# Weight sums of a seven-product MLP made by adding DMAs, with a new order of products, loads and last sums

## The chip, the cores and the metric

The kernel runs on one core of one Trainium2 chip. The metric is the device time of one execution in microseconds (us); the kernel before takes 2369.47 us in the median of three runs. A core has five engines that run their own instruction streams in order and signal each other by semaphores: TensorE (PE, with PEld for its weight loads), VectorE (DVE), ScalarE (ACT), GpSimd (POOL) and SyncE (SP), which here only issues DMAs.

## The reference

Two layers of a decoder over 1024 tokens of width 1024 in float32. Each layer is a mixer (RG-LRU and retention in layer 0, HGRN2 and gated DeltaNet in layer 1) and then an MLP, both behind an RMSNorm with adaLN shift, scale and gate. The change concerns the two MLPs alone:

```python
def squared_relu_mlp(h, w1, w2):
    return jnp.square(jax.nn.relu(h @ w1)) @ w2

    # in each layer, after the mixer:
    h = modulate(rmsnorm(x, norm_mlp_w[layer]), sh_f, sc_f)
    x = x + gt_f[:, None, :] * squared_relu_mlp(h, mlp_w1[layer], mlp_w2[layer])
```

`w1` is 1024 x 4096, `w2` is 4096 x 1024. The result is x after both layers and a last RMSNorm.

## The kernel before

**Order of the work.** Nothing is issued as it is written. A `Recorder` collects every operation with its engine, an assumed duration and the tiles that it reads and writes; `place()` then plays a list schedule over all of it (per engine the ready operation with the lowest priority number, which is its place in the text plus the `bias` in force), gives each tile a buffer, and `emit()` (L333, the call itself is L342, hence one line in all rows of the profile) issues each engine's operations in that order. So what is fixed on the chip is the order per engine and the buffers; a wait at the head of an engine's stream holds up all behind it. Pools: `heap` (73 tiles of 128 x 512), `raw` (4 of 128 x 1024, loaded weights), `w` (6 of 128 x 1024, split weights), `pad` (4 of 128 x 515), `blk` (3), and in PSUM `dps` (3 banks) and `psum` (5 banks). `raw`, `w`, `blk`, `pad` and `dps` are handed out in the order of the text. All DMAs go out on SP's queue (`dma`, L476).

**Precision.** Every factor is split in two float32r tiles: hi is ScalarE's rounded copy, lo the remainder, which VectorE (or GpSimd) forms by a subtraction. A product of two factors is three matmuls: hi x hi, hi x lo, lo x hi (`mm3`, and the same written out in the MLP). `factor` (L597) splits a weight block into one `w` buffer, `operand` (L791) an activation tile into two heap tiles.

**The MLP** (`mlp`, L854). Both products are done by the seven-product scheme of Strassen and Winograd for 2 x 2 blocks: seven block products, named P1 to P7, in place of eight, with sums of blocks before and after. The tokens are cut in two halves (f = 0, 1) and the inner dimension in two; the 4096 hidden channels are 32 units of 128, taken as 16 pairs (`NP`).

- *Up* (first product). `winograd_operands` (L823) forms seven sets of four activation operands, 56 heap tiles: P1 and P2 from the first half of the tokens alone, the others from sums of both halves. `up(s, kind)` (L865) is one product: 12 matmuls of 128 x 512. P2 accumulates on P1's PSUM bank, P3 on P5's and P4 on P7's. VectorE and ScalarE form the four results (r11, r22, r12, r21) of a pair from them, apply ReLU and square, form the second product's sums t1, r, t2 and t4 of them, and spill seven tiles per pair to DRAM (`h_spill`). `mlp_plan` (L675) orders the products: P1 of the first three pairs (`LEAD`), P2 of these, their other five, then pair by pair, the last two pairs interleaved.
- *Down* (second product). `todo` (L933) goes over groups of four pairs (`GRP`), over the kinds in `DOWN_ORDER` (P1 P2 P6 P7 P4 P5 P3), over the pairs of the group; each step is again 12 matmuls, into four PSUM banks that accumulate over the four pairs. At the end of a kind, its four banks are added into x (`add_to`, L950) or into four shared tiles in two `blk` buffers, which are added into x at the very end (`last_adds`, L953). `load_h` (L937) brings the spilled tiles back six steps ahead.

**Weights.** `units` lists all weight units in the order of use; `pop` keeps three of them pushed ahead, at a priority before everything else. For the up product, `up_factor` (L619) loads two tiles of 128 x 1024 per pair into `raw` (blocks a11, a12 and a21, a22), and GpSimd forms the block sums that P5, P6, P7 and P3 need: x = a21 + a22 in a `pad` tile, then x - a11, a11 - a21, a12 - x. For the down product, `load_w` (L942) loads four blocks per pair for a whole group at once, and `down_factor` (L643) forms the same four sums on GpSimd, which there also forms the lo parts of P7, P4 and P3.

`pop` also feeds, among the up units of the first MLP, loads of adaLN weights into `raw` tiles and their multiplication on VectorE (`ada_unit`, L729), whose results the second layer needs.

The tiles of x are spilled before the MLP and loaded again in four batches of four by `X_LOADS` (L443, used at L990).

## Time and profile before

| | |
|---|---|
| runs, us | 2365.61, 2370.98, 2369.47 (median 2369.47) |
| the profiled execution's own time, us | 2369.33 |
| its span in the profile, us | 2367.6 |
| mean granted TensorE clock | 0.987 of full |
| DMA queues | one data queue, SP's: 336.80 MB in 168964 packets, 43.6% of 16 engines' span |

The stages of interest, by the trace: first MLP from about 452 us (its last operands are still being formed) to the seam between up and down at 780 to 787 us, and on to about 1090; second MLP from about 1715 us over the seam at 2032.6 to 2039.9 us to about 2347; then the last norm and the stores.

How to read the rows. A group's row gives line, engine, operation, the tile written and the tiles read, shapes and count, then busy time in us, mean duration of one in ns, and after the second bar the idle time of the engine just before these instructions, with the engines that ended it. In the timeline a row is a run of like instructions: start, length, engine, what, count, and in brackets the idle time ahead of it. In the table of windows each engine's busy time stands with its count of instructions, then granted clock, DMA share of 16 engines, GB/s. Matmuls overlap, so a matmul's mean of some 390 ns is longer than the distance between two. A few per cent of the matmul records are missing from the trace.

### The profile page before, as it was taken

Reading aid. Unit: us, or ns where it says so; the run is one execution under the profiler, and the core shown is the slowest. Engines: PE = TensorE matmul, PEld = TensorE weight load, DVE = VectorE, ACT = ScalarE, POOL = GpSimd, SP = SyncE. Lnnn points to the kernel's source line nnn. Section 1 sums busy time; section 2 is a strip of 40 time slices with the busy share of each in tenths; the row PEclk is TensorE's granted clock in tenths of the full one; section 3 lists DMA queues with packets and bytes.
Section 4 is the critical chain, followed back from the end, with each engine's and each line's share of the span. In section 5 each row is a group of like instructions: output and inputs, shape, how many; then the busy total and the mean of one; then the engine's idle time right before and its main releaser. Section 6 shows DMA issues by size and latency. Waiting matters only on the chain.

```text
span 2367.6 us, 31238 instructions
## 1 busy us (share of the span) xinstructions
PE 2291.4 (97%) x10906; PEld 1872.5 (79%) x10906; DVE 1835.2 (78%) x2719; ACT 1270.4 (54%) x2372; POOL 749.0 (32%) x695
## 2 busy tenths in 40 slices
PE   7999999999999899999999999999989999899997
PEld 4887888777778788887887888888868888788885
DVE  7997666798886788789977686656697665787787
ACT  6786463654445434445755665555465445444443
POOL 3000000123244356531164444520033332466541
PEclk8999999999999999999999999999999999999998
DMA  8333426237776845324212122234325445764431
GB/s 288 89 107 107 125 89 231 98 122 267 256 246 230 306 154 178 105 96 138 75 36 76 60 62 65 57 110 150 126 76 191 147 147 195 273 203 134 138 98 72
DMA packets 169122, 338.80 MB, mean 143 GB/s; under 512 B 26818, under 2 KB 37634, under 8 KB 168964
## 3 DMA queue, kind: packets, MB, share of 16 engines
q1 hardware_dynamic: 168964, 336.80, 43.6%
q8 instruction: 86, 1.41, 0.2%
q14 instruction: 72, 0.59, 0.1%
HBM read 254.39 MB, written 82.35 MB: 142 GB/s over the span
## 4 chain that ended last, share of the span: by engine, by line
PE 77%; DVE 9%; issue 5%; DMA 4%; ACT 4%; POOL 1%; SPq 0%; DVEq 0%; POOLq 0%; ACTq 0%
PE dps L342 41%; PE psum L342 36%; DVE heap L342 6%; ACT heap L342 3%; DMA raw<-in_dram 2%; DVE w L342 2%; DMA heap<-in_dram 1%; DVE raw L342 1%; POOL pad L342 1%; POOL raw L342 1%; ACT w L342 1%; DMA h_spill<-heap 0%; DMA d_full<-blk 0%; SPq L342 0%; DMA heap<-d_full 0%
## 5 line engine op out<-in xcount | busy, mean ns | idle before, releaser
L342 PE MATMUL dps<-heap,w 128*128 128x512 f32 x5016 | 1246.4, 395 | 5.8 <-ACT heap L342 2.8
L342 PEld LDWEIGHTS dps<-heap,w 128*128 128x128 f32 x5016 | 927.1, 188 | 197.5 <-ACT heap L342 5.2
L342 PE MATMUL psum<-heap,w 128*128 128x512 f32 x3816 | 906.4, 393 | 33.2 <-DVE heap L342 22.1
L342 PEld LDWEIGHTS psum<-heap,w 128*128 128x128 f32 x3816 | 720.8, 190 | 195.5 <-DVE heap L342 24.4
L342 DVE TENSOR_TENSOR heap<-heap,heap 128x512 f32<-128x512 f32 (+1 forms) x799 | 654.6, 847 | 90.7 <-ACT heap L342 86.4
L342 ACT ACTIVATE heap<-heap 128x512 f32<-128x512 f32 (+2 forms) x1055 | 613.6, 608 | 176.7 <-DVE heap L342 161.6
L342 ACT ACTIVATE w<-raw 128x512 fp32r<-128x512 f32 (+1 forms) x312 | 233.2, 750 | 351.2 <-PE psum L342 180.6
L342 DVE TENSOR_TENSOR w<-raw,w 128x512 fp32r<-128x512 f32 (+1 forms) x309 | 294.2, 955 | 106.2 <-ACT w L342 101.3
L342 POOL TENSOR_TENSOR pad<-raw 128x512 f32<-128x512 f32 x32 | 44.5, 1391 | 779.0 <-ACT w L342 399.0
L342 ACT ACTIVATE w<-heap 128x512 fp32r<-128x512 f32 x160 | 101.2, 632 | 242.7 <-PE psum L342 240.0
L342 POOL TENSOR_TENSOR w<-heap,w 128x512 fp32r<-128x512 f32 x96 | 137.7, 1437 | 199.7 <-ACT w L342 196.2
L342 POOL TENSOR_TENSOR blk<-blk,blk 32x31 f32<-32x31 f32 (+15 forms) x248 | 177.0, 714 | 37.2 <-DMA blk<-n_full 19.7
L342 DVE TENSOR_TENSOR heap<-psum,heap 128x512 f32<-128x512 f32 x153 | 103.7, 684 | 42.1 <-PE psum L342 41.3
L342 ACT ACTIVATE heap<-psum 128x512 f32<-128x512 f32 (+6 forms) x189 | 89.6, 481 | 82.0 <-PE psum L342 80.9
L342 PE MATMUL psum<-heap,heap 128*128 128x128 f32 (+4 forms) x1064 | 129.9, 263 | 2.2 <-DVE heap L342 2.2
L342 PEld LDWEIGHTS psum<-heap,heap 128*128 128x128 f32 (+2 forms) x1064 | 112.5, 168 | 23.5 <-DVE heap L342 5.6
L342 DVE SCALAR_TENSOR_TENSOR raw<-raw,blk 128x1024 f32<-128x1024 f32 x80 | 100.9, 1261 | 29.3 <-DMA raw<-in_dram 28.8
L342 DVE SCALAR_TENSOR_TENSOR heap<-dps,mod,heap 128x512 f32<-128x512 f32 x80 | 57.4, 747 | 55.3 <-PE dps L342 55.3
L342 POOL TENSOR_TENSOR pad<-pad,raw 128x512 f32<-128x512 f32 x32 | 51.0, 1595 | 135.8 <-DVE w L342 135.8
L342 ACT ACTIVATE heap<-dps 128x512 f32<-128x512 f32 (+1 forms) x134 | 77.5, 585 | 24.5 <-PE dps L342 14.9
L342 DVE SCALAR_TENSOR_TENSOR heap<-psum,mod,heap 128x512 f32<-128x512 f32 x112 | 78.6, 744 | 14.9 <-PE psum L342 14.7
L342 DVE TENSOR_TENSOR w<-pad,w 128x512 fp32r<-128x512 f32 x64 | 63.1, 987 | 33.3 <-ACT w L342 32.8
(174 smaller groups left out, 1533.6 us busy)
## 6 DMA issues: line engine op xcount, KB each, us to landing
raw<-in_dram SPq DMA_DIRECT2D x232, 512.0 KB, 3.7
h_spill<-heap SPq DMA_DIRECT2D x224, 256.0 KB, 3.4
heap<-h_spill SPq DMA_DIRECT2D x224, 256.0 KB, 2.9
heap<-in_dram SPq DMA_DIRECT2D x194, 256.0 KB, 5.4
x_spill<-heap SPq DMA_DIRECT2D x48, 256.0 KB, 2.0
heap<-x_spill SPq DMA_DIRECT2D x48, 256.0 KB, 5.3
heap<-g_rows SPq DMA_DIRECT2D x16, 256.0 KB, 4.4
out_dram<-heap SPq DMA_DIRECT2D x16, 256.0 KB, 2.7
```

What stands on the lines that cost most here:

```text
L342: op.call(*a, **k)
```

## The change

- **Adding DMAs.** A new helper `dma_add` issues a DMA from GpSimd's queue that adds what it reads in DRAM to the destination tile in SBUF. In the up product, per pair: a21 is loaded into the `pad` tile x by SP, a22 is added to it (P5); a21 and a22 are loaded into `raw`, a11 is added to the first (P7); a11 is added to x after P5's split has read it (P6); a12 is added to x after P6's split (P3). That is four adding DMAs and one more plain load of 256 KB per pair; GpSimd's four additions go. In the down product, a21 + a22 and a21 + a11 are formed by adding DMAs while loading (five tiles per pair in place of four), and two additions stay on GpSimd. A DMA can add but not subtract, so the scheme's first block row is taken with the other sign: some sums after the products become differences, P3's weights are split negated, and `gn` holds the negated gate.
- **All lo parts on VectorE.** `factor` no longer takes an engine.
- **Second product over 8 pairs.** `GRP` is 8: two groups of eight pairs, so PSUM is read out half as often.
- **Five pairs ahead.** `mlp_plan` begins with P1 of five pairs (`AHEAD`), then P2 of these; their a11 and a12 are loaded as separate half tiles.
- **Weights and x one by one.** `W_LOADS` names the step of a group at which each block of each pair is loaded (from eight steps before the group on), `X_LOADS` the step for each tile of x.
- **Last sums of results later.** The sums t1, r, t2, t4 of the last two pairs, and their spills, get a priority 300 places later.
- The last sums of the shared tiles into the second half of x come after P7 of the last group instead of after P4.

The diff, cut to its core:

```diff
-GRP = 4
+GRP = 8
+LATER = 300
-X_LOADS = {(0, 1): (0, 0), (1, 3): (1, 4), (2, 3): (0, 4), (3, 3): (1, 0)}
+X_LOADS = {i + n * m: (f, k + m) for i, n, f, k in ((2, 2, 0, 0), (23, 2, 1, 4), (32, 1, 0, 4), (40, 1, 1, 0)) for m in range(4)}
+W_LOADS = {(i + n * j, name): j for i, n, name in ((-8, 1, "a11"), (0, 1, "a12"), (1, 2, "x"), (10, 2, "a21"), (24, 1, "a22"))
+           for j in range(GRP)}
+AHEAD = 5
+    def dma_add(o, i, after=()):
+        n = 8 * width(o) * o.shape[0]
+        views = [x for x in (i, o) if isinstance(x, View)]
+        return rec.add("POOL", nc.gpsimd.dma_start, 800, (o, i), dict(accum_op=ALU.add), [o], views, after, n)
...
-    def factor(src, eng):
+    def factor(src, negative=False):
         w = rec.tile("w", F32R)
         hi, lo = w[:, 0:HT], w[:, HT:D]
-        act(hi, src, AF.Copy)
-        eng.tensor_tensor(lo, src, hi.bitcast(F32), ALU.subtract)
+        if negative:
+            act(hi, src, AF.Copy, scale=-1.0)
+            V.scalar_tensor_tensor(lo, src, -1.0, hi.bitcast(F32), ALU.mult, ALU.subtract)
+        else:
+            act(hi, src, AF.Copy)
+            V.tensor_tensor(lo, src, hi.bitcast(F32), ALU.subtract)
         return hi, lo
...
     def up_factor(l, s, kind, pw):
+        a11, a12 = w_1[l, 2 * s][:, 0:HT], w_1[l, 2 * s][:, HT:D]
+        a21, a22 = w_1[l, 2 * s + 1][:, 0:HT], w_1[l, 2 * s + 1][:, HT:D]
         def get():
+            if s < AHEAD and kind in ("P1", "P2"):
+                r = rec.tile("raw")[:, 0:HT]
+                dma(r, a11 if kind == "P1" else a12)
+                return factor(r)
             if kind == "P1":
-                pw["r"] = r = rec.tile("raw")
+                r = rec.tile("raw")
                 dma(r, w_1[l, 2 * s])
-                pw["a11"], pw["a12"] = r[:, 0:HT], r[:, HT:D]
+                pw["P1"], pw["P2"] = r[:, 0:HT], r[:, HT:D]
             if kind == "P5":
+                pw["x"] = padded()[:, 0:HT]
+                dma(pw["x"], a21)
+                dma_add(pw["x"], a22)
                 r = rec.tile("raw")
                 dma(r, w_1[l, 2 * s + 1])
-                pw["a21"], pw["a22"] = r[:, 0:HT], r[:, HT:D]
-                pw["x"] = padded()[:, 0:HT]
-                G.tensor_tensor(pw["x"], pw["a21"], pw["a22"], ALU.add)
...
+                pw["P7"], pw["P4"] = r[:, 0:HT], r[:, HT:D]
+                dma_add(pw["P7"], a11)
             if kind == "P6":
-                G.tensor_tensor(x, x, a11, ALU.subtract)
-            if kind == "P7":
-                G.tensor_tensor(a21, a11, a21, ALU.subtract)
+                dma_add(pw["x"], a11)
             if kind == "P3":
-                G.tensor_tensor(a12, a12, x, ALU.subtract)
...
+                dma_add(pw["x"], a12)
+            return factor(pw.get(kind, pw.get("x")), kind == "P3")
...
     def mlp_plan():
-        r = [(s, k) for k in ("P1", "P2") for s in range(LEAD)]
+        r = [(s, k) for k in ("P1", "P2") for s in range(AHEAD)]
...
             elif kind == "P3":
                 relu2(r)
-                t1 = ht("t")
...
+                with bias(LATER if s >= NP - 2 else 0):
+                    t1 = ht("t")
+                    V.tensor_tensor(t1, r, p["r11"], ALU.subtract)
...
+        def load_block(g, j, n):
+            pw, s = down_pw[l, g][j], 2 * (GRP * g + j)
+            a11, a12 = (w_2[l, s + i][:, 0:HT] for i in range(2))
+            a21, a22 = (w_2[l, s + i][:, HT:D] for i in range(2))
+            with bias(-2 * BIG):
+                pw[n] = ht("w2")
+                dma(pw[n], {"a11": a11, "a12": a12, "a21": a21, "a22": a22, "x": a21}[n], [marks[-1]])
+                if n == "a21":
+                    dma_add(pw[n], a11)
+                if n == "x":
+                    dma_add(pw[n], a22)
...
+            load_w(g, n % (7 * GRP))
+            load_w(g + 1, n % (7 * GRP) - 7 * GRP)
```

More of the change, by code (lines that the diff above doesn't have):

```diff
@@ L181, in add @@
         op.seq, op.group = len(self.ops), self.group
-        op.port = eng in ("DVE", "POOL") and sum(
+        op.port = not nbytes and eng in ("DVE", "POOL") and sum(
             v.buf.pool not in ("psum", "dps") and width(v) > 64 for v in ins) > (eng == "DVE")
@@ L645, in get @@
             if kind == "P6":
-                r = rec.tile("raw")
-                pw["x"], pw["y"] = r[:, 0:HT], r[:, HT:D]
-                G.tensor_tensor(pw["x"], pw["a21"], pw["a22"], ALU.add)
-                G.tensor_tensor(pw["y"], pw["x"], pw["a11"], ALU.subtract)
-            a11, a12, a21, a22, x, y = (pw.get(n) for n in ("a11", "a12", "a21", "a22", "x", "y"))
-            if kind == "P7":
-                G.tensor_tensor(a21, a11, a21, ALU.subtract)
-            if kind == "P4":
-                G.tensor_tensor(a12, a12, y, ALU.subtract)
-            src = {"P1": a11, "P2": a12, "P5": x, "P6": y, "P7": a21, "P3": a12, "P4": a22}[kind]
-            return factor(src, V if kind in ("P1", "P2", "P6", "P5") else G)
+                G.tensor_tensor(pw["a11"], pw["a11"], pw["x"], ALU.add)
+            if kind == "P7":
+                G.tensor_tensor(pw["a12"], pw["a12"], pw["a11"], ALU.add)
+            n = {"P1": "a11", "P2": "a12", "P5": "x", "P6": "a11", "P7": "a21", "P3": "a12", "P4": "a22"}[kind]
+            return factor(pw[n], kind == "P3")
         return get
@@ L883, in relu2 @@
                 if kind != "P2":
-                    act(r, r, AF.Relu)
+                    act(r, r, AF.Relu, scale=-1.0 if kind == "P3" else 1.0)
                 act(r, r, AF.Square)
@@ L989, in mlp @@
                 xh = [[None] * KC, [None] * KC]
-            if (n // 4, n % 4) in X_LOADS:
-                f, k0 = X_LOADS[n // 4, n % 4]
-                for k in range(k0, k0 + 4):
-                    xh[f][k] = ht("x")
-                    dma(xh[f][k], xs[k, :, f * HT:(f + 1) * HT], [marks[-1]])
-            if kind == "P2" and j == 0 and g + 1 < NP // GRP:
-                load_w(g + 1, ("a11", "a12", "a21", "a22"))
+            if n in X_LOADS:
+                f, k = X_LOADS[n]
+                xh[f][k] = ht("x")
+                dma(xh[f][k], xs[k, :, f * HT:(f + 1) * HT], [marks[-1]])
+            load_w(g, n % (7 * GRP))
+            load_w(g + 1, n % (7 * GRP) - 7 * GRP)
             if j < GRP - 1:
@@ L1011, in mlp @@
                     last_adds(0, range(4, 8))
-                if kind == "P4":
+                if kind == "P7":
                     last_adds(1, range(8))
```

74 lines of the change are left out of this document (36 added, 38 removed).

## The prediction

> **What bounds the kernel now.** I read the page's totals first, then the table of windows for the two MLPs, then TensorE's timeline inside the windows that are not full, and last the groups by form for VectorE, GpSimd and the DMA.
>
> ```profile
> span 2367.6 us, 31238 instructions
> PE 2291.4 (97%) x10906; PEld 1872.5 (79%) x10906; DVE 1835.2 (78%) x2719; ACT 1270.4 (54%) x2372; POOL 749.0 (32%) x695
> ```
>
> TensorE is the bound. The change keeps every matmul (each MLP still has 112 products of 12 matmuls up and 112 down), so it can only win back time in which TensorE stands. Where that is, the windows show: stretch, length, busy us of PE, PEld, DVE, ACT and POOL with counts, granted clock, DMA share, GB/s.
>
> ```profile
> 452.20:486.00 33.80, 28.04 (x104) 20.83 (x102) 29.56 (x38) 24.33 (x44) 12.82 (x8) 0.90 0.18 63
> 486.00:530.00 44.00, 43.18 (x185) 34.33 (x186) 42.55 (x58) 22.28 (x40) 12.76 (x8) 1.00 0.42 130
> 530.00:700.00 170.00, 162.23 (x705) 131.28 (x705) 149.96 (x208) 80.68 (x141) 57.59 (x35) 1.00 0.80 262
> ...
> 780.10:787.30 7.20, 0.00 (x0) 0.00 (x0) 7.20 (x12) 3.90 (x8) 1.27 (x1) 0.79 0.62 229
> 787.30:1080.00 292.70, 292.66 (x1283) 242.21 (x1284) 240.41 (x290) 126.74 (x220) 145.86 (x101) 0.99 0.52 170
> 1715.20:1748.90 33.70, 27.96 (x104) 20.86 (x102) 30.76 (x37) 24.29 (x44) 12.10 (x8) 0.90 0.19 62
> 1748.90:2032.60 283.70, 282.63 (x1241) 232.39 (x1241) 196.16 (x258) 148.91 (x261) 97.95 (x67) 1.00 0.47 162
> 2032.60:2039.85 7.25, 0.00 (x0) 0.00 (x0) 7.25 (x12) 3.92 (x8) 1.27 (x1) 0.80 0.62 229
> 2039.85:2335.00 295.15, 295.15 (x1294) 244.23 (x1295) 242.76 (x294) 127.27 (x222) 145.19 (x98) 0.99 0.48 154
> ```
>
> Both down stages (787.30 on, 2039.85 on) are full: nothing done there can gain. TensorE loses time at the start of each up stage, at the seam between up and down, and, in the first MLP alone, 170 - 162.23 = 7.8 us in 530 to 700, where adaLN's weight tiles are loaded and multiplied besides.
>
> **Part 1: five pairs ahead.** The up stage begins with P1 and P2 of three pairs, which need only the first half of the tokens; P5, P6, P7 need both.
>
> ```profile
> 457.75 9.91 PE L342 MATMUL dps<-heap,w 128*128 128x512 f32 x43
> 468.80 0.50 PE L342 MATMUL psum<-heap,w 128*128 128x512 f32 x1 [1.14 <-ACT heap L342]
> 470.84 5.50 PE L342 MATMUL psum<-heap,w 128*128 128x512 f32 x17 [1.54 <-ACT w L342]
> 477.52 0.73 PE L342 MATMUL psum<-heap,w 128*128 128x512 f32 x2 [1.18 <-ACT heap L342]
> 479.20 5.39 PE L342 MATMUL psum<-heap,w 128*128 128x512 f32 x14 [0.95 <-ACT heap L342]
> 485.11 0.50 PE L342 MATMUL psum<-heap,w 128*128 128x512 f32 x1 [0.52 <-ACT heap L342]
> 486.03 16.93 PE L342 MATMUL psum<-heap,w 128*128 128x512 f32 x73 [0.43 <-DVE heap L342]
> ```
>
> The pace of a product at full speed, and the seam:
>
> ```profile
> 751.82 5.60 PE L342 MATMUL dps<-heap,w 128*128 128x512 f32 x24
> 757.26 22.83 PE L342 MATMUL psum<-heap,w 128*128 128x512 f32 x100
> 787.34 12.92 PE L342 MATMUL psum<-heap,w 128*128 128x512 f32 x48 [7.26 <-DVE heap L342]
> ```
>
> 24 matmuls start 5.44 us apart (751.82 to 757.26), so a product takes 2.72. The first block of P1 and P2 ends at 457.75 + 9.91 = 467.66, and TensorE is back in stride at 486.03. In those 18.4 us it did 1 + 17 + 2 + 14 + 1 = 35 matmuls, three products or 8.2 us: 10.2 us are lost, waiting on operands that ScalarE and VectorE are still splitting (VectorE is busy 29.56 of 33.80 us in this window). Two pairs more give four products more, 4 x 2.72 = 10.9 us of work that waits for none of it, just over the loss. They are not free of VectorE: four weight splits move ahead, some 0.7 us each. But this window also holds 8 GpSimd operations that go away (part 3). I take 9.5 us back and leave 0.7 for the small waits at its end. The second MLP has the same window (27.96 of 33.70 busy, the same 104 matmuls): 2 x 9.5 = 19.0 us. The cover that this needs is buffer space: five pairs hold ten unfinished tiles of the heap of 73 beside the 56 of operands. If it is short, the four products come no earlier, and the gain falls to what two of them cover, about 5 per MLP.
>
> **Part 2: last sums later.** At the seam TensorE waits 7.26 us for VectorE.
>
> ```profile
> 781.09 9.20 DVE L342 TENSOR_TENSOR heap<-heap,heap 128x512 f32<-128x512 f32 x14
> ```
>
> ```profile
> L342 DVE TENSOR_TENSOR heap<-heap,heap 128x512 f32<-128x512 f32 x8 | 5.6, 766 | 0.0
> ```
>
> The second row is the groups by form for 781.5 to 786.4: the first eight of those fourteen are f32, the t1, r, t2, t4 of the last two pairs (4 x 2), and only the fp32r splits of the first down operands come behind them. The bias of 300 moves the eight behind splits that are written later, and their eight spill DMAs on SP's queue with them; that queue then reaches the next loads sooner. Their results are read in the second group of eight pairs, over 56 products later, so nothing waits. 5.4 of the 7.26 us go (the rest is the last eviction and one split); the first six or so matmuls after such a stand run slow (48 in 12.92 us against 10.9 at the pace), and half of that, 1 us, goes too. 2 x 6.4 = 12.8 us. What is late next is the eviction of the last P4.
>
> **Part 3: adding DMAs in place of GpSimd.**
>
> ```profile
> L342 DVE TENSOR_TENSOR w<-raw,w 128x512 fp32r<-128x512 f32 x224 | 189.0, 849 | 71.9 <-ACT w L342 71.8
> L342 ACT ACTIVATE w<-raw 128x512 fp32r<-128x512 f32 x224 | 140.1, 629 | 243.3 <-PE psum L342 176.7 <-PE dps L342 49.5 <-issue 13.2
> ...
> L342 DVE TENSOR_TENSOR w<-pad,w 128x512 fp32r<-128x512 f32 x64 | 63.1, 987 | 33.3 <-ACT w L342 32.8
> ...
> L342 POOL TENSOR_TENSOR pad<-raw 128x512 f32<-128x512 f32 x32 | 44.5, 1391 | 779.0 <-ACT w L342 399.0 <-DMA raw<-in_dram 362.7 <-DVE heap L342 17.2
> ```
>
> ```profile
> L342 DVE TENSOR_TENSOR w<-raw,w x309: 672/693/1778, 71.2 to 2319.8; 128x512 fp32r<-128x512 f32 x112, 128x1024 fp32r<-128x1024 f32 x43
> ```
>
> The first rows are groups (busy us, mean ns, idle before); the last is the same split seen tile by tile, minimum, median and maximum. The split takes 0.67 us at best and 0.85 (from raw) or 0.99 (from pad) in the mean: it slows where a GpSimd addition of 1.4 us runs beside it. All four additions of a pair go in the up stage, so VectorE's 149.96 of 170 us shrink, and the 7.8 us at 530 to 700, the 0.8 before and the 1.1 in the second MLP are no longer VectorE's to lose.
>
> What comes in: per pair one plain load (a21 into pad) and four adding DMAs of 256 KB, issued from GpSimd's queue. The trace of before has no DMA from GpSimd and none that adds. Two questions: latency and engine time.
>
> Latency. P6 and P3 now wait for an add that itself waits for the split before it. A weight is split as soon as one of six w buffers is free: ScalarE's idle time ahead of the splits was ended by TensorE, 176.7 + 49.5 of 243.3 us, not by a load. So a split stands five products, 13.6 us, ahead of its use. From P5 to P6 and from P6 to P3 are two products each, 5.4 us.
>
> ```profile
> 2040.00:2080.00 40.00, 40.00 (x169) 32.94 (x170) 25.97 (x36) 15.23 (x27) 12.32 (x10) 0.95 1.03 368
> ```
>
> ```profile
> raw<-in_dram SPq DMA_DIRECT2D x232, 512.0 KB, 3.7
> ...
> heap<-in_dram SPq DMA_DIRECT2D x194, 256.0 KB, 5.4
> ```
>
> ```profile
> L342 DVE SCALAR_TENSOR_TENSOR raw<-raw,blk 128x1024 f32<-128x1024 f32 x40 | 52.0, 1301 | 17.4 <-DMA raw<-in_dram 17.1
> ```
>
> An add that lands like the slowest plain kind, 5.4 us, plus the two splits at 0.6 and 0.7, falls 1.3 us behind the 5.4, twice a pair: 2.6 of 13.6 us, and the next pair's P1 starts afresh. Hidden. The cover is used up only if an add takes about 11 us from issue to landing. Queued behind a late add are, on GpSimd, only other adds, but on ScalarE and VectorE, which run in order, the evictions that free PSUM.
>
> Engine time. Only 530 to 700 is near its limit: 262 GB/s at a share of 0.80, so a share of 1 is 328 GB/s and 256 KB take 0.80 us of all engines. The most that any 40 us of the trace reached is the first row above, 1.03 and 368 GB/s. The window has 170 / 19.04 = 8.9 pairs. The plain load adds 8.9 x 0.80 / 170 = 0.042. An add reads its destination too, so it costs once to twice a plain load (three times as a far bound): 0.168, 0.335, 0.50. Shares: 1.01, 1.18, 1.34. Against 1.03 that is nothing lost at once; at twice 170 x 1.18 / 1.03 = 195 us, 25 more; by bytes at 368 GB/s it is (44.5 + 2.3 + 18.7) MB or 178 us, 8 more. In between, one and a half: 180 us by share, 165 by bytes. I take the middle of these two, a window 2.5 us longer than now, so that the 7.8 us are not won, and VectorE's wait for adaLN's loads (17.1 us in the last row) grows. Bounds: -7.8 and +51 us (1.34 / 1.03).
>
> The Trainium skill, page "DMA: Bandwidth & Descriptors", section "Issuing engines are not separate DMA queues", speaks against the change: DMAs from any engine interleave on the same 16 engines, so a queue of its own gives no bandwidth. By its table of measured transfers, which gives 0.95 us for 64 KB and 6.15 for 1 MB, I would estimate 2 us for 256 KB, and the window would lie beyond even the share at twice. No run here shows an add yet.
>
> **Part 4: second product over 8 pairs, loads one by one.**
>
> ```profile
> L342 POOL TENSOR_TENSOR w<-heap,w 128x512 fp32r<-128x512 f32 x96 | 137.7, 1437 | 199.7 <-ACT w L342 196.2 <-DVE heap L342 2.2 <-DMA heap<-h_spill 1.3
> ...
> L342 DVE SCALAR_TENSOR_TENSOR heap<-psum,mod,heap 128x512 f32<-128x512 f32 x112 | 78.6, 744 | 14.9 <-PE psum L342 14.7
> ```
>
> Evictions per MLP fall from 112 to 56: 56 x 0.744 = 41.7 us off VectorE. The 48 splits per MLP that GpSimd did come to it: 48 x 0.69 = 33. It stays at about 235 of 293 us under a full TensorE: 0 gained, 0 lost. Two adds and one more load per pair raise the DMA share from 0.52 by (16 + 32 x 2) x 0.80 / 293 = 0.22 at twice: below 1, and blocks are loaded seven or more steps (19 us) ahead. Two GpSimd additions per pair stay, at 1.4 us in 38 us. The sign changes replace operations one for one. Cost if this cover goes (a block late): 2.72 us per product. The last sums into x move from after P4 to after P7, both before the last evictions: 0.
>
> **The sum.** The profiled run took 2369.33 us, 1.7 outside its span, 0.1 from the median of the runs. 19.0 + 12.8 + 0.8 + 1.1 - 2.5 = 31.2 off: **2338 us**. Its own range: all of the starts, seams and windows back would be 2 x 10.2 + 2 x (7.26 + 1) + 9.7 = 47 off, 2323; the adds at twice instead, by shares, 9 off, 2360.
>
> **Rivals.**
>
> *The adds bind adaLN's window (slower).* Place: 530 to 700 of the first MLP. If an add takes three times a plain load, the window is 221 us, 51 more, and with the other parts won (33.7) the time is 2369.3 - 33.7 + 51 = 2387. It turns the sign from the point where the window passes 170 + 33.7 us: share 1.03 x 203.7 / 170 = 1.234, so adds at (1.234 - 0.842) / 0.168 = 2.3 times a plain load. For it: the share of 0.80, and the 17.1 us. Against: reading twice and writing once has no third part, and adaLN's loads may slip later, for they are needed only after the MLP.
>
> *The start doesn't fill.* VectorE is the bound of the start rather than the order of products (29.56 of 33.80, then 42.55 of 44.00 us busy), or the heap is short; each start gives 5 instead of 9.5, and the adds' splits hold up ScalarE now and then: 31.2 - 9 - 3 = 19 off, 2350.
>
> *It does nothing that counts.* Adds at just over twice eat what starts and seams give: 2365 to 2374, about 2368.
>
> **How the numbers follow.** Forecast 0.60, the start unfilled 0.16, nothing 0.08, slower 0.16. The range 2323 to 2374 takes in the ceiling, the first two cases and the third; it leaves out the slower one and little else. Two tenths of a per cent, 4.7 us, is about what a measurement of this kernel can tell. Faster by more 0.76, within 0.07, slower 0.17.
>
> **What would show it.** Right: TensorE unbroken from P1 to P5 at each MLP's start; at most 2 us at each seam, with fp32r splits ahead of the f32 results; 64 adds per MLP in the up stages and 32 in the down stages on GpSimd's queue; the split from raw near 0.69 us; down stages as long as now. Wrong: waits of ScalarE on pad or raw landings that stop TensorE in 530 to 700 with a DMA share near 1; gaps in a down stage; the gap at the start only moved behind the extra products.

## The result, and the profile after

The changed kernel takes 2393.79 us (median of four runs, 2387.70 to 2397.86), the kernel before 2370.05 us in the runs beside it: a ratio of 1.0102, 95% interval 1.0076 to 1.0127. It is slower, by about 24 us, where 31 us less were forecast, and it lies above the range. The profiled execution took 2387.7 us.

From the page of the kernel after, the totals:

```profile
span 2385.9 us, 31550 instructions
PE 2299.5 (96%) x10906; PEld 1878.8 (79%) x10906; DVE 1667.2 (70%) x2705; ACT 1266.7 (53%) x2372; POOL 475.8 (20%) x599
```

The matmuls are the same 10906. VectorE has 168 us less to do and GpSimd 273 us less, and the span is 18.3 us longer all the same: the bound is not work but waiting. Where, the windows of the kernel after tell (stretch, length, busy us of PE, PEld, DVE, ACT, POOL with counts, granted clock, DMA share, GB/s):

```profile
456.70:530.00 73.30, 65.72 (x275) 52.24 (x274) 61.58 (x99) 45.38 (x81) 13.95 (x16) 0.95 0.85 216
530.00:700.00 170.00, 165.82 (x717) 134.99 (x717) 127.70 (x209) 83.19 (x146) 29.72 (x34) 0.99 1.01 311
700.00:780.30 80.30, 77.73 (x341) 63.42 (x340) 45.70 (x77) 42.21 (x75) 8.71 (x10) 1.00 0.80 232
780.30:1080.00 299.70, 297.72 (x1313) 243.79 (x1312) 224.31 (x309) 139.03 (x242) 73.13 (x68) 1.00 0.71 216
...
1748.90:2059.00 310.10, 280.36 (x1170) 227.00 (x1169) 157.04 (x244) 140.84 (x248) 43.76 (x50) 0.96 0.70 185
2059.00:2335.00 276.00, 274.52 (x1207) 226.05 (x1206) 200.14 (x276) 122.37 (x214) 72.48 (x64) 1.00 0.73 218
```

One row stands out: 1748.9 to 2059, the second MLP's up stage, where TensorE stands for 30 of 310 us (before: 1.1 of 283.7). The adaLN stretch 530 to 700, with the DMA engines full at 1.01, lost less than before (4.2 us against 7.8), and the down stages are full but for one short stand each.

To compare kernels I cut each run at two marks: the up stage begins at the first of the two column-sum matmuls of the norm (`psum<-heap,ones_r`) that TensorE does just before the MLP, and ends where the first down product starts (reckoned back from VectorE's first reading of its bank, at 2.72 us per product of the group).

| us | first up stage | second up stage | between them | after the second | span |
|---|---|---|---|---|---|
| before | 331.2 | 320.9 | 931.7 | 328.1 | 2367.6 |
| after | 323.6 | 348.6 | 930.1 | 326.9 | 2385.9 |
| difference | -7.6 | +27.7 | -1.6 | -1.2 | +18.3 |

(The first mark itself came 1.0 us later.) The change gave 7.6 us in the first up stage and lost 27.7 in the second, with the same up product in both (the first has adaLN's work besides). TensorE's timeline of after in the second (start, length, what, count, idle time ahead of it):

```profile
1820.19 3.04 PE L342 MATMUL dps<-heap,w 128*128 128x512 f32 x12 [2.46 <-ACT heap L342]
...
1841.05 3.03 PE L342 MATMUL dps<-heap,w 128*128 128x512 f32 x12 [1.51 <-ACT heap L342]
...
1865.47 5.40 PE L342 MATMUL dps<-heap,w 128*128 128x512 f32 x12 [5.06 <-ACT heap L342]
1870.71 11.07 PE L342 MATMUL psum<-heap,w 128*128 128x512 f32 x48
...
1889.56 4.22 PE L342 MATMUL dps<-heap,w 128*128 128x512 f32 x12 [2.35 <-ACT heap L342]
...
1913.50 4.22 PE L342 MATMUL dps<-heap,w 128*128 128x512 f32 x12 [2.92 <-ACT heap L342]
```

From 1820 on TensorE stops once per pair for eight pairs, 21 to 24 us apart where seven products take 19.0, always at the same product: the twelve matmuls into `dps` just before a run of 48. In the order P1 P5 P2 P6 P7 P3 P4 that is P2, which accumulates on P1's bank and must wait until ScalarE has copied P1 out. So the engine named, ScalarE, is late with a copy of 0.58 us. The timeline of all engines over one such pair, cut to the chain:

```profile
1844.79 0.69 DVE L342 TENSOR_TENSOR w<-pad,w 128x512 fp32r<-128x512 f32 x1 [2.05 <-ACT w L342]
...
1849.11 0.86 POOL L342 DMA_DIRECT2D raw<-in_dram  x1 [5.18 <-DMA raw<-in_dram]
...
1849.64 1.22 POOL L342 DMA_DIRECT2D pad<-in_dram  x1
1854.80 2.88 PE L342 MATMUL dps<-heap,w 128*128 128x512 f32 x12
1856.45 0.63 ACT L342 ACTIVATE w<-pad 128x512 fp32r<-128x512 f32 x1 [8.98 <-DMA pad<-in_dram]
1857.52 2.88 PE L342 MATMUL psum<-heap,w 128*128 128x512 f32 x12
...
1862.60 0.63 ACT L342 ACTIVATE w<-pad 128x512 fp32r<-128x512 f32 x1 [1.29 <-DMA pad<-in_dram]
...
1864.84 0.58 ACT L342 ACTIVATE heap<-dps 128x512 f32<-128x512 f32 x1
```

P5's split of the next pair has read x by 1845.48. The add for P6 could start then, but ahead of it on GpSimd's queue stands the add for P7, which waits for its raw tile until 1849.11; P6's add goes out at 1849.64 and has landed at 1856.4, 11 us after the split that released it. All that time, 8.98 us, ScalarE stands at the head of its stream on the split for P6. That split is not late for its own product (P6 starts at 1870.71, 14 us on). But written behind it are the splits for P7, P3 and P4, six passes over results, and only then the copy of P1, whose product ended at about 1857.5: it starts at 1864.84, and TensorE, after P5, has stood for 5.06 us. The split for P3 in between waits for a second add, which could only start when P6's split had read x.

### The profile page after: what moved, and what is told of

Read it like the earlier page. It is cut to its first block, busy times and chain, and to the rows that moved or that the text cites. A ratio compares the mean times of both kernels' runs of the same rounds, so it can differ in the third digit from the quotient of the medians.

```text
span 2385.9 us, 31550 instructions
## 1 busy us (share of the span) xinstructions
PE 2299.5 (96%) x10906; PEld 1878.8 (79%) x10906; DVE 1667.2 (70%) x2705; ACT 1266.7 (53%) x2372; POOL 475.8 (20%) x599
## 3 DMA queue, kind: packets, MB, share of 16 engines
q0 software_dynamic: 27648, 50.34, 12.9%
## 4 chain that ended last, share of the span: by engine, by line
PE 73%; DMA 14%; DVE 5%; ACT 5%; issue 3%; POOL 0%; SPq 0%; DVEq 0%; ACTq 0%; POOLq 0%
PE dps L342 41%; PE psum L342 32%; DMA pad<-in_dram 10%; ACT heap L342 3%; DVE heap L342 3%; DVE w L342 2%; DMA raw<-in_dram 2%; DMA heap<-in_dram 2%; ACT w L342 1%; DVE raw L342 1%; DMA h_spill<-heap 1%; DMA heap<-h_spill 0%; POOL raw L342 0%; ACT L342 0%; SPq L342 0%
## 5 line engine op out<-in xcount | busy, mean ns | idle before, releaser
L342 DVE TENSOR_TENSOR heap<-heap,heap 128x512 f32<-128x512 f32 (+1 forms) x799 | 561.6, 726 | 82.0 <-ACT heap L342 76.1
L342 ACT ACTIVATE w<-heap 128x512 fp32r<-128x512 f32 x224 | 140.5, 630 | 274.7 <-PE psum L342 204.7
L342 ACT ACTIVATE w<-raw 128x512 fp32r<-128x512 f32 (+1 forms) x216 | 171.0, 799 | 170.6 <-PE dps L342 112.3
L342 DVE TENSOR_TENSOR w<-heap,w 128x512 fp32r<-128x512 f32 x192 | 162.2, 851 | 110.2 <-ACT w L342 110.0
L342 DVE TENSOR_TENSOR w<-raw,w 128x512 fp32r<-128x512 f32 (+1 forms) x213 | 190.8, 905 | 64.3 <-ACT w L342 54.3
L342 POOL DMA_DIRECT2D pad<-in_dram x96 | 87.7, 921 | 516.9 <-DVE w L342 332.2
L342 ACT ACTIVATE w<-pad 128x512 fp32r<-128x512 f32 x96 | 60.3, 628 | 186.5 <-DMA pad<-in_dram 146.2
L342 POOL DMA_DIRECT2D raw<-in_dram x32 | 28.3, 883 | 567.4 <-DMA raw<-in_dram 491.8
L342 POOL TENSOR_TENSOR heap<-heap,heap 128x512 f32<-128x512 f32 x71 | 108.2, 1535 | 107.5 <-DVE w L342 57.1
L342 POOL DMA_DIRECT2D heap<-in_dram x64 | 60.0, 1010 | 235.8 <-DVE heap L342 128.0
```

Source lines behind the costliest of these rows:

```text
L342: op.call(*a, **k)
```

## The experiments

Two theories, and a third that the diff suggests:

- **A, the order behind the wait.** `place()` reckons that any DMA has landed 2.0 us after its transfer. For an adding DMA that is too early, so ScalarE's fixed order has splits that wait for adds ahead of copies that free PSUM. The loss should go with the assumed landing alone, with nothing else changed, and go away where the adds land sooner or are not chained.
- **B, engine time.** The adds take the 16 DMA engines so long that transfers bind the stages, whatever the order.
- **C, another part.** Five pairs ahead, the late sums, the second product over 8 pairs or the lo parts on VectorE cost the time.

All medians, with the ratio to before and its interval, and the two up stages of the profiled execution:

| | median us | ratio, 95% | up 1 | up 2 |
|---|---|---|---|---|
| before | 2369.17 to 2372.69 beside the runs | 1 | 331.2 | 320.9 |
| after | 2393.79 | 1.0102 [1.0076, 1.0127] | 323.6 | 348.6 |
| adds assumed later, 5.0 us | 2419.79 | 1.0204 [1.0189, 1.0219] | 378.8 | 316.7 |
| adds assumed earlier, 0.5 us | 2428.48 | 1.0242 [1.0221, 1.0263] | 328.9 | 372.2 |
| plain copies for adds | 2336.68 | 0.9857 [0.9840, 0.9873] | 305.4 | 315.1 |
| plain copies, more loads | 2369.75 | 0.9995 [0.9983, 1.0008] | 316.0 | 335.1 |
| up sums by GpSimd | 2370.47 | 0.9995 [0.9986, 1.0005] | 335.3 | 318.8 |
| before, ahead and later | 2381.12 | 1.0044 [1.0029, 1.0060] | 339.5 | 322.4 |
| before, later alone | 2362.17 | 0.9956 [0.9941, 0.9971] | 328.2 | 317.2 |
| later landing in the second MLP | 2353.80 | 0.9931 [0.9905, 0.9957] | 319.6 | 313.5 |
| two adds per pair | 2349.04 | 0.9901 [0.9884, 0.9917] | 322.4 | 309.9 |
| two adds, three ahead | 2346.99 | 0.9905 [0.9889, 0.9922] | 321.3 | 307.8 |
| adds later, counted once | 2396.12 | 1.0108 [1.0091, 1.0124] | 357.1 | 318.6 |
| after, three ahead | 2391.07 | 1.0091 [1.0076, 1.0106] | 321.4 | 351.7 |

112 products of 2.72 us are 304.6 us, so about 305 is an up stage with nothing lost.

**The adds' landing in the planner, later.** The same operations; only the order in which they are written changes.

```diff
-                    op.end = dma_free + 2000.0
+                    op.end = dma_free + (5000.0 if e == "POOL" else 2000.0)
```

> The changed kernel with one number of its planner altered: an adding DMA is assumed to land 5.0 us after its transfer instead of 2.0, so that the order of the engines' streams allows for it; no operation is added or removed. Theory A (the loss of the second up stage is PSUM copies of P1 and P5 that stand in ScalarE's stream behind splits which wait for an adding DMA, and the order assumes the add some 3 us too early): the second up stage comes back from 352 us to 325 to 330, the time to 2355 to 2372. Rival B (what adding DMAs cost is time of the 16 DMA engines or of GpSimd): order does not matter, 2385 to 2400. Rival C (the products are put in a worse order by five pairs ahead, eight pairs or the single loads): 2385 to 2400 too.

The second up stage went from 348.6 to 316.7, as theory A wants, but the first from 323.6 to 378.8, and the kernel is slower still. The largest of TensorE's waits in the first up stage of this run (waiting line, awaited engine, us in total, times, longest):

```profile
PE psum L342 <- ACT w L342: 30.8, 12, 4.0
```

Here TensorE waits for the splits themselves, not for a copy: with all adds assumed late, the planner wrote splits of the first MLP too late. So the total, which lies outside every range that was expected, settles nothing, and the stages answer in opposite directions.

**The adds' landing, earlier.** The same line with 500.0 in place of 5000.0.

> The same number altered the other way: an adding DMA is assumed to land 0.5 us after its transfer instead of 2.0. Theory A: splits that wait for adds stand further ahead in ScalarE's stream, more copies behind them, 10 to 30 us slower than the changed kernel, 2400 to 2425. Rivals B and C: no change beyond a few us, 2385 to 2400.

The second up stage grows to 372.2, the first stays near (328.9). From 0.5 over 2.0 to 5.0 us the second stage takes 372, 349 and 317: one assumed number, no instruction more or less, and a steady answer. TensorE's waits for ScalarE's `heap` copies in it rise with the loss: `dps` 32.7 us here, 24.0 in after, 0.2 with 5.0 us.

**Plain copies in place of adds.** The six sums per pair that adding DMAs make are left out: each GpSimd DMA overwrites its tile.

```diff
-        return rec.add("POOL", nc.gpsimd.dma_start, 800, (o, i), dict(accum_op=ALU.add), [o], views, after, n)
+        return rec.add("POOL", nc.gpsimd.dma_start, 800, (o, i), {}, [o], views, after, n)
```

> The changed kernel with GpSimd's DMAs as plain copies of the same bytes in the same order: the block sums are left out, the destination is overwritten. Theory A: what counts is when such a DMA lands; if the adding itself is what makes it land late (5.5 to 6.7 us against 3.0 to 3.5 for a plain one of 256 KB into the same tiles from SyncE), 2 to 3 us earlier landings win back most, 2345 to 2365; if it is GpSimd's way of issuing, it stays at 2380 to 2395. Rival B (engine time, 1.6 us of all engines per add against 0.8): halved, 2345 to 2365 as well, with a DMA share in the second up stage lower by 0.15. Rival C: no change, 2385 to 2400.

The first stage is at its least, 305.4, the second at 315.1, and the kernel takes 2336.68. Every engine issues the same instructions in the same order as in after (31550 in both), so everything that the change loses against before hangs on the adds being slower than copies. Queue and landing rows, after first and then with plain copies (packets, MB, share of 16 engines; KB, median us from issue to landing):

```profile
q0 software_dynamic: 27648, 50.34, 12.9%
...
pad<-in_dram POOLq DMA_DIRECT2D x96, 256.0 KB, 5.9
heap<-in_dram POOLq DMA_DIRECT2D x64, 256.0 KB, 6.7
```

```profile
q0 software_dynamic: 15360, 50.34, 6.6%
...
pad<-in_dram POOLq DMA_DIRECT2D x96, 256.0 KB, 4.5
heap<-in_dram POOLq DMA_DIRECT2D x64, 256.0 KB, 5.6
```

GpSimd's queue has 192 DMAs: 12.9% of 2385.9 us is 307.8, or 1.60 us of all engines for an add; 6.6% of 2332.1 is 153.9, or 0.80 for a copy. An add takes twice the engine time and lands 1.1 to 1.4 us later. This run changes both, so it doesn't part A from B.

**Up sums by GpSimd again**, all else as after. (The first five pairs load the whole tile of a11 and a12 again at P5, which this form needs.)

```diff
-                pw["x"] = padded()[:, 0:HT]
-                dma(pw["x"], a21)
-                dma_add(pw["x"], a22)
...
-                dma_add(pw["P7"], a11)
+                pw["x"] = padded()[:, 0:HT]
+                G.tensor_tensor(pw["x"], pw["P7"], pw["P4"], ALU.add)
             if kind == "P6":
-                dma_add(pw["x"], a11)
+                G.tensor_tensor(pw["x"], pw["x"], pw["P1"], ALU.add)
+            if kind == "P7":
+                G.tensor_tensor(pw["P7"], pw["P7"], pw["P1"], ALU.add)
             if kind == "P3":
-                dma_add(pw["x"], a12)
+                G.tensor_tensor(pw["x"], pw["x"], pw["P2"], ALU.add)
```

> The changed kernel with the up product's block sums made by GpSimd again (additions in the new signs; for the first five pairs the tile with a11 and a12 is loaded once more at P5). Everything else of the change stays, the adding DMAs of the down product too. Theories A and B: the second up stage falls to 313 to 320 us, the first to about 320, the time to 2335 to 2352, as the prediction's parts 1 and 2 had it. Rival C: the second up stage stays near 350 us, the time at 2380 or more.

The loss in the second stage is gone (318.8) and the time is that of before, 2370.47. So the 28 us come from the up product's adds and not from the second product over 8 pairs, its adds or the lo parts on VectorE: theory C falls for these. But 2335 to 2352 was expected, with a first stage of about 320, and that one takes 335.3. The gain at the seams is in here too, so something else takes about as much: the start, as the next two show.

**Parts 1 and 2 put on the kernel before.**

```diff
+LATER = 300
+AHEAD = 5
...
+            if s < AHEAD and kind in ("P1", "P2"):
+                r = rec.tile("raw")[:, 0:HT]
+                dma(r, w_1[l, 2 * s][:, 0:HT] if kind == "P1" else w_1[l, 2 * s][:, HT:D])
+                return factor(r, V)
-            if kind == "P1":
+            if kind == ("P5" if s < AHEAD else "P1"):
...
-        r = [(s, k) for k in ("P1", "P2") for s in range(LEAD)]
+        r = [(s, k) for k in ("P1", "P2") for s in range(AHEAD)]
...
+                with bias(LATER if s >= NP - 2 else 0):
```

> The kernel before with parts 1 and 2 of the change alone: five pairs ahead (their a11 and a12 loaded as half tiles, and the whole tile once more at P5, since GpSimd still makes the sums) and the last sums 300 places later. Groups of four, loads and GpSimd's sums as before. By the prediction's terms 19.0 and 12.8 us off: 2338 to 2345. Rival D (VectorE is the bound of the start, so that products done ahead only move the stand behind them): the seam alone is won, 2352 to 2362.

**Part 2 alone on the kernel before:** only `LATER` and the two `with bias(LATER if s >= NP - 2 else 0)` blocks of the lines above.

> The kernel before with the last sums of the last two pairs 300 places later, nothing else. By the prediction's term 12.8 us off, TensorE's wait at each seam from 7.26 to 2 us or less: 2355 to 2361. If the wait at the seam has another cause that stands behind it (the last eviction, the reload of the spilled tiles): under 5 us off, 2365 to 2372.

Later sums alone take 2362.17 against 2371.56, 9.4 us off; TensorE's stand at the first seam goes from 7.26 us to this:

```profile
784.25 11.72 PE L342 MATMUL psum<-heap,w 128*128 128x512 f32 x44 [2.44 <-DVE heap L342]
```

With five pairs ahead as well it is 2381.12: 19 us worse, not 19 better. TensorE's timeline of that run at the start of the first MLP:

```profile
479.45 6.81 PE L342 MATMUL psum<-heap,w 128*128 128x512 f32 x25
486.76 1.33 PE L342 MATMUL psum<-heap,w 128*128 128x512 f32 x3 [0.50 <-DVE heap L342]
490.32 0.50 PE L342 MATMUL psum<-heap,w 128*128 128x512 f32 x1 [2.23 <-ACT heap L342]
491.46 17.07 PE L342 MATMUL psum<-heap,w 128*128 128x512 f32 x67 [0.64 <-DVE heap L342]
514.81 5.57 PE L342 MATMUL psum<-heap,w 128*128 128x512 f32 x14 [6.28 <-DVE heap L342]
```

P1 and P2 run on for twenty us with stands of 0.2 us, and then TensorE waits again, 3.4 us in three stands (the longest for ScalarE), 6.28 for VectorE some twenty us later, and 5.09 at 530.47. (Five tiles of 512 KB per MLP are loaded twice in this form; that share of the 19 us was not measured apart.)

**A later landing for the second MLP's up adds alone.**

```diff
-                    op.end = dma_free + 2000.0
+                    op.end = dma_free + 2000.0 + op.late
...
+        late = 3000.0 * l
...
-                dma_add(pw["x"], a22)
+                dma_add(pw["x"], a22, late=late)
...
-                dma_add(pw["P7"], a11)
+                dma_add(pw["P7"], a11, late=late)
...
-                dma_add(pw["x"], a11)
+                dma_add(pw["x"], a11, late=late)
...
-                dma_add(pw["x"], a12)
+                dma_add(pw["x"], a12, late=late)
```

> The changed kernel with the planner's assumption of later landings (5.0 instead of 2.0 us) for the adding DMAs of the second up stage alone. Theory A, as the first two runs left it (order decides, each way, in the second up stage; in the first, where the planner already reckons with loaded DMA queues, later landings only hurt): second up stage 315 to 322 us, first as in the changed kernel 322 to 328, time 2352 to 2368. If the gain of the second stage in the run with all adds late came from the other order of the first: no gain, 2385 or more.

2353.80, 40 us below after. The second up stage takes 313.5 with the same adds on the same engines (q0's share 12.8%, median landing in `pad` 6.0 us). This decides between A and B for the second stage: the engine time is unchanged and the loss is gone. What changed is the order. ScalarE's timeline of this run over one pair:

```profile
1853.25 0.58 ACT L343 ACTIVATE heap<-dps 128x512 f32<-128x512 f32 x1
1854.53 0.63 ACT L343 ACTIVATE w<-pad 128x512 fp32r<-128x512 f32 x1 [0.70 <-DMA pad<-in_dram]
...
1862.25 0.63 ACT L343 ACTIVATE w<-pad 128x512 fp32r<-128x512 f32 x1 [2.85 <-DMA pad<-in_dram]
```

(The line number is one higher for the added lines.) The copy of P1 (1853.25) now stands ahead of both splits that wait for a chained add, P6's (1854.53) and P3's (1862.25), where in after it stands behind both. TensorE's wait for copies out of `dps`, over the second up stage:

```profile
PE dps L343 <- ACT heap L343: 0.2, 1, 0.2
```

The first up stage of after has by itself an order in between; its ScalarE timeline:

```profile
600.24 0.63 ACT L342 ACTIVATE w<-pad 128x512 fp32r<-128x512 f32 x1 [3.12 <-DMA pad<-in_dram]
...
605.18 0.58 ACT L342 ACTIVATE heap<-dps 128x512 f32<-128x512 f32 x1
...
606.39 0.63 ACT L342 ACTIVATE w<-pad 128x512 fp32r<-128x512 f32 x1
```

The copy of P1 (605.18) stands behind P6's split (600.24) but ahead of P3's (606.39). So the first stage was hit less, not spared: TensorE's waits for copies out of `dps` come to 6.5 us there, against 24.0 in the second stage and 0.7 in the first with plain copies. The reason may be that adaLN's loads fill the planner's account of the DMA there, so that it puts the landings, and with them the splits, later. (The order is seen in the trace; that adaLN's loads are what makes it was only argued.)

**Two adds per pair.** a22 into x (P5) and a11 into the raw tile (P7) stay adding DMAs; the two that depend on an earlier split, x + a11 and x + a12, go back to GpSimd (with a11 and a12 of the first five pairs loaded again at P5, as above).

```diff
             if kind == "P6":
-                dma_add(pw["x"], a11)
+                G.tensor_tensor(pw["x"], pw["x"], pw["P1"], ALU.add)
             if kind == "P3":
-                dma_add(pw["x"], a12)
+                G.tensor_tensor(pw["x"], pw["x"], pw["P2"], ALU.add)
```

> The changed kernel with two of the four adding DMAs per pair of the up product: a22 into x and a11 into P7's block, which wait for no split. x + a11 and + a12, which stand between two splits, are additions on GpSimd again (a11 and a12 kept in raw, loaded once more for the first five pairs). Theory A: no copy stands behind a split that waits for an add in series; up stages 312 to 325 us, time 2335 to 2358. Rival B (time of the DMA engines): half of the loss of the second stage stays, 2365 to 2382. GpSimd's two additions per pair slow VectorE's splits less than four did.

2349.04, and 309.9 us for the second up stage. Theory B had half of the loss stay. An add that waits for nothing but a load can be issued early; the harm came with the chained ones. TensorE's wait for copies out of `dps`, over the second up stage of this run, is down from 24.0 us in after to this:

```profile
PE dps L342 <- ACT heap L342: 0.2, 1, 0.2
```

**Later landing, bytes of an add counted once.** The adds' landing at 5000.0 as in the first experiment, and in `dma_add` half the bytes on the planner's account of the DMA:

```diff
-        n = 8 * width(o) * o.shape[0]
+        n = 4 * width(o) * o.shape[0]
```

> The run with all adds assumed late (5.0 us) with one more number of the planner altered: the bytes of an add are counted once, not twice, in its model of the DMA queues. That run's first up stage took 379 us against 324 in the changed kernel. Theory A (only the order decides; the planner's own DMA queues were full where adaLN's tiles are loaded, and 5 us more pushed the splits so late that TensorE waits for weights): with the queues relieved the first up stage comes to 310 to 335 us, the second stays at 314 to 322, the time at 2342 to 2372. Rival B (engine time): as the run before, 2400 to 2420.

The first up stage takes 357.1, not the 310 to 335 expected: TensorE's wait for ScalarE's `w` there falls from 30.8 to 14.0 us, and 22 of the 55 us come back. The time, 2396.12, lies between the ranges of the two theories. So the double count is part of why the planner errs in the first MLP; the rest of that loss stays open.

**Two adds and three pairs ahead**, and **the change as it is with three pairs ahead:**

```diff
-AHEAD = 5
+AHEAD = 3
```

> The run with two adds per pair (2349 us) with three pairs ahead instead of five. By the prediction's part 1, two pairs more are worth 9.5 us per MLP: 2360 to 2370. If the products done ahead only move TensorE's stand to behind them (in that run 4.7 us each, waiting on VectorE): within 5 us of it, 2344 to 2354.

> The changed kernel with three pairs ahead instead of five, so part 1 undone. By the prediction's part 1: 19 us slower than the changed kernel, 2405 to 2418. Rival C (five pairs ahead is what costs): faster, 2365 to 2385. If it only moves the stand: 2385 to 2400.

2346.99 against 2349.04 with two adds, 2391.07 against 2393.79 with four: the two more pairs gain nothing in either. TensorE's timelines at the first MLP's start, with four adds and three pairs ahead, then with plain copies and five:

```profile
473.25 30.02 PE L342 MATMUL psum<-heap,w 128*128 128x512 f32 x124 [4.69 <-ACT heap L342]
503.77 10.80 PE L342 MATMUL psum<-heap,w 128*128 128x512 f32 x44 [0.50 <-ACT heap L342]
```

```profile
511.61 38.39 PE L342 MATMUL psum<-heap,w 128*128 128x512 f32 x168 [2.33 <-DVE heap L342]
```

With three pairs ahead the start now stands 5.2 us, where before lost 10.2 (counted by the pace; by the pace these two rows lose 5.3). With five and copies it stands 2.3. Of the kernels that compute the whole reference the two with two adds are the fastest, 22 us below before.

**Plain copies with as many loads again**, to give the engines the time back that the adds took, and no sums: each GpSimd DMA is a plain copy, as above, and SP issues 192 more copies of 256 KB, from the same blocks into DRAM that nobody reads.

```diff
-        return rec.add("POOL", nc.gpsimd.dma_start, 800, (o, i), dict(accum_op=ALU.add), [o], views, after, n)
+        op = rec.add("POOL", nc.gpsimd.dma_start, 800, (o, i), {}, [o], views, after, n)
+        rec.add("SP", nc.sync.dma_start, 60, (extra[count[0]], i), {}, [], [], [op], 0)
```

> The run with plain copies in place of adds (2337 us, sums left out), and behind each of the 192 copies one more DMA of the same 256 KB from SyncE into scratch DRAM, for which nothing waits. The DMA engines then carry at least as much as with adds (a share of about 0.13 more over the span), while landings that something waits for stay plain. Theory A (an add costs by landing late ahead of splits): 2333 to 2350. Rival B (time of the DMA engines): back to 2375 to 2400.

Both theories missed: 2369.75. The second up stage takes 335.1, between 315.1 without the loads and 348.6 with adds, and the landings lie between as well:

```profile
pad<-in_dram POOLq DMA_DIRECT2D x96, 256.0 KB, 5.5
```

4.5, 5.5 and 5.9 us of landing go with 315, 335 and 349 us of stage, in one and the same plan: the other engines issue the same instructions in the same order in all three. TensorE's waits for copies out of `dps` in that stage go along, 8.5, 16.6 and 24.0 us. (The extra copies also stand in SyncE's stream, each behind a GpSimd DMA; what they hold up there was not measured apart.) So engine time does matter, but by way of the landing that ScalarE waits for; with an order that allows for that landing (313.5 us above) it costs next to nothing. Theory A holds with this amendment.

## Why the prediction was wrong, point by point

**The step that failed** is the latency in part 3: "Hidden. The cover is used up only if an add takes about 11 us from issue to landing." The cover was worked out for the product that uses the split, and for that it held: the split for P6 at 1856.45 was 14 us early, and in the eight pairs with a stop the add for P6 landed 4.4 to 7.5 us after its issue, always under the 11. TensorE stopped all the same. The prediction went on to name what else is queued behind a late add, "on ScalarE and VectorE, which run in order, the evictions that free PSUM", and gave it no price. That price is 35.1 us in the second stage (348.6 against 313.5 with the order mended), more than the 27.7 that the stage lost on balance. The copy of P1 has a cover of one product, P5, 2.7 us; ScalarE, which had stood for 8.98 us until 1856.45, reached it 7.3 us after P1's end. The prediction's sign of failure, "waits of ScalarE on pad or raw landings that stop TensorE in 530 to 700", named the right wait; it came in the second MLP instead, at a DMA share of 0.70. The waits in that stage, first TensorE's, then ScalarE's:

```profile
PE dps L342 <- ACT heap L342: 24.0, 9, 5.1
PE psum L342 <- ACT heap L342: 7.3, 4, 3.6
```

```profile
ACT w L342 <- DMA pad<-in_dram: 92.8, 24, 9.0
```

The latency itself was also short by two terms: the 5.4 us taken for an add measured 5.9 to 6.7 in the median, and the prediction let each add start when its tile was free, where in these eight pairs P6's add went out 0.4 to 4.2 us after that, behind P7's add on GpSimd's queue (in the pair shown, one whose raw tile had not landed). In the pair shown the two make 11 us from split to split, in the other seven 4.9 to 9.9. The prediction had said that only other adds are queued behind a late one on GpSimd; that was so, and it was not harmless.

**Part 1, 19.0 us, measured about 0.** "About 0" is five pairs against three, with two adds and with four. As predicted, TensorE runs almost unbroken from P1 to P5 (timeline of after, first MLP, and one row of VectorE's):

```profile
464.58 15.90 PE L342 MATMUL dps<-heap,w 128*128 128x512 f32 x67 [0.19 <-ACT heap L342]
480.32 8.10 PE L342 MATMUL psum<-heap,w 128*128 128x512 f32 x35
489.42 2.11 PE L342 MATMUL psum<-heap,w 128*128 128x512 f32 x8 [1.01 <-DVE heap L342]
492.54 20.94 PE L342 MATMUL psum<-heap,w 128*128 128x512 f32 x89 [1.00 <-DVE heap L342]
515.49 1.22 DVE L342 SCALAR_TENSOR_TENSOR raw<-raw,blk 128x1024 f32<-128x1024 f32 x1 [2.06 <-DMA raw<-in_dram]
518.67 40.65 PE L342 MATMUL psum<-heap,w 128*128 128x512 f32 x168 [5.20 <-DVE heap L342]
```

But then it stands 7.2 us in three places (in the second MLP 3.7, also in three, up to 1788): the gap moved behind the extra products, which the prediction listed as a sign against it. Two things were left out. The loss that the extra products were to cover was itself halved by the rest of the change, part 3 most likely: with three pairs ahead the start stands 5.2 us now. (The prediction saw that GpSimd's eight operations leave this window, and did not take that off the 10.2.) And VectorE's readings of PSUM, which the products behind P1 and P2 wait for, stand behind other work in its stream. In the longest stand VectorE was not full, as the rival "the start doesn't fill" had it, but stood for 2.06 us itself, on a load of adaLN (515.49), with two such readings behind. With landings of copies five pairs ahead leave a stand of 2.3 us; whether three would do as well there was not tried. With GpSimd's sums they cost time.

**Part 2, 12.8 us, measured 9.4.** The mechanism was right, the size a little off: 2.44 us of either stand stay where 1.9 were allowed, and little of the 1 us per seam for slow matmuls was won: behind the stand of 2.44 us six matmuls still start 0.43 us apart, where the pace is 0.23 and before had seven. In after the stand at the seam is gone, TensorE's timeline passes over it (1.96 us of waiting for ScalarE come 21 us later):

```profile
757.48 43.68 PE L342 MATMUL psum<-heap,w 128*128 128x512 f32 x192
```

**Part 3, contention: right.** VectorE's split from `pad` fell to its best time (group of after):

```profile
L342 DVE TENSOR_TENSOR w<-pad,w 128x512 fp32r<-128x512 f32 x64 | 44.2, 691 | 104.6 <-ACT w L342 104.4
```

987 ns before, 691 now, and 889 in the changed kernel with GpSimd's sums put back. With copies in place of adds the first stage runs at 305.4 us; with adds it keeps 323.6, so what VectorE gives the landings take back in part.

**Part 3, engine time: the price right, the place wrong.** An add costs 2.0 times a plain load, inside the bounds of once to three times. But the window 530 to 700 did not grow by 2.5 us; TensorE did 3.6 us more work in it. The prediction held the added load against the window alone, as if adaLN's loads had to stay there. Weighted by length, the share of the whole first up stage is 0.92 in the windows above ((73.3 x 0.85 + 170 x 1.01 + 80.3 x 0.80) / 323.6): the demand fits the stage, and the loads spread into its neighbours. So the rival "the adds bind adaLN's window" gave 2387, near the result, for a reason that the runs refute. The Trainium skill, page "DMA: Bandwidth & Descriptors", section "Issuing engines are not separate DMA queues", bears on what did happen: all queues interleave on the same 16 engines, and here 192 more copies on SP's queue made GpSimd's into `pad` land 1.0 us later (4.5 to 5.5; those into `heap` stayed at 5.6), so the trace agrees. The prediction's estimate from that page, 2 us for 256 KB, is above both prices measured, 1.60 us of the engines for an add and 0.80 for a copy.

**Part 4, 0: right.** From the first down product to the second MLP 930.1 us against 931.7, after the second up stage 326.9 against 328.1.

With the order mended for the second MLP alone the change takes 2353.80 us. Of the terms in the 16 us that are left to the forecast, part 1 is the largest that was not found: 19.0 forecast, about 0 measured; the rest was not taken apart. That plain copies come to 2336.68, next to the forecast of 2338, is chance: they win 25.8 us in the first stage, where the terms have 14.2, and 5.8 in the second, where they have 17.0.

## What to carry to other kernels

When an engine's operation is replaced by a DMA, count its landing against everything that stands behind the waiting instruction in its engine's stream, and against the shortest cover among them, not against the cover of the tile that lands. Where a planner fixes the order, its assumed latency is part of the kernel: one number moved a 320 us stage by 24 us one way and 32 the other, so a new kind of DMA needs its measured landing there before it is judged. Additions that depend only on loads were the good candidates for adding DMAs here; those chained behind a consumer's reading need an order that allows for their landing (313.5 us with it, 348.6 without, 309.9 with GpSimd doing them).

## What the runs showed of the hardware that was not expected

- **A busy DMA at a share of 1.0 cost TensorE little.** In 530 to 700 the engines were at 1.01 and 311 GB/s, and TensorE worked 165.82 of 170 us; the price was in landings: the adds into `pad` landed after 7.2 us there in the median, after 5.2 in the second up stage.
- **What an adding DMA costs.** 1.60 us of all 16 engines for 256 KB against 0.80 for a copy, in 144 packets against 80, and a landing after 5.9 and 6.7 us in the median against 4.5 and 5.6 for copies from the same queue in the same plan.
- **A short stop can cost more than its length.** Twelve matmuls without a stop ahead of them have a length of 2.88 us (1854.80). After a stop of 1.51 us they took 3.03, after 2.35 or 2.92 us 4.22, after 5.06 us 5.40, but after 2.46 us only 3.04 (1820.19). Of the seven stops over 2 us in those pairs six cost 1.3 to 2.5 us more behind them and one 0.2. The granted clock (third number from the right) goes along:

```profile
1820.19:1823.07 2.88, 2.88 (x13) 2.36 (x14) 0.96 (x2) 0.95 (x2) 0.00 (x0) 1.00 0.99 289
1889.56:1893.58 4.02, 4.02 (x13) 3.16 (x13) 1.70 (x3) 0.96 (x2) 0.87 (x1) 0.69 1.02 322
```

In the clock's record of this run half speed comes in one or two stretches of 3.41 us. Within the two MLPs TensorE had stood for 1.79 us or more in the 3.41 us just before each of them, and for 1.73 at most in any that full speed followed. The stop of 2.46 us fell on two such stretches, with 1.72 and 0.75 us; that of 2.35 us had 1.85 us in one. So it matters how a stop falls, not its length alone. (The bound is of this run; in before 1.4 us were enough twice.) The Trainium skill, page "TensorE: Matmul & The Clock Gate", section "What's actually happening", has the clock at half once TensorE has been idle for a window of about 3.4 us. Twice 2.88 is 5.76, and the row after the longest stop comes near; but stops shorter than that window slowed it here too.
